# Gating values of a token mixer by seven block products instead of eight half products, with the spatial gate moved one stage later

## The chip, the cores and the metric

The kernel runs on one core of a Trainium2 chip. The metric is the device time of one execution in microseconds, the median of several runs. All matrix products work on 32-bit floats that are split into a high and a low part of the type fp32r ("hi" and "lo"), so that each product of two tiles is three matmuls: hi x hi, hi x lo and lo x hi.

## What is computed

The reference is one layer of a token mixer and a convolutional feed-forward part, for 512 tokens of width 1024 and 256 context tokens. What matters here is the token mixer, and in it u, vs and r:

```python
hx = _modulate(_rms_norm(x, norm1_g[l]), sh1x, sc1x)
z = h @ w_in
u, vs, q, r, ga, gb, k, v, lr = _split(z, IN_SPLITS)
a = _spatial_gating(gelu(u), gelu(vs), sgu_ln_g, sgu_ln_b, sgu_w, sgu_b)
...                                   # o: gated linear attention of q, k, v
ob = o.astype(h.dtype) * jax.nn.silu(r)
merged = sigmoid(ga) * (a @ w_br_a) + sigmoid(gb) * (ob @ w_br_b)

def _spatial_gating(u, vs, ln_g, ln_b, w_s, b_s):
    vn = _layer_norm(vs, ln_g, ln_b).reshape(bsz, n, SGU_CHUNK, SGU_GROUPS, SGU_GROUP_DIM)
    s = jnp.einsum('gpq,bnqgc->bnpgc', w_s, vn) + b_s.T[:, :, None]
    return u * s.reshape(bsz, length, SGU_WIDTH)
```

vs, r, ga and gb are each a product of the modulated x (512 x 1024) with 1024 columns of w_in (1024 x 1024). u is one too, but it is wanted with its channels on the partitions.

## The kernel before, in words

**Stages.** After the context's products and the products for q, k and v, the stages that matter here follow each other in this order: vs, u, the r gate, the ga gate, the gb gate, the product with w_br_a (also called a gate), the product with w_br_b, w_o, and the feed-forward part. The attention of four heads is cut into steps that run as hooks between the matmuls (`hook`, L1021); those of heads 2 and 3 run beside vs.

**Weights.** All weights come as a stream of units in the list `specs`: a unit is 512 KB, either all 1024 rows by 128 columns (u) or 256 rows by 512 columns (the others). `weights()` (L267) hands out the next unit. Its load on SP's queue goes to one of five raw buffers (RAW, L41); ACT casts it to its high part (L249) and DVE subtracts to get the low part (L250), into one of five pairs. So up to ten units can be ahead of the PE.

**vs** (`wide_tm`, L411, called at L1175): two halves of 512 columns, each with four token tiles of 128, eight blocks of the inner dimension and three matmuls of 128x512; 192 matmuls and eight units. `vs_done` (L1163) applies Gelu and collects the statistics of the layer norm. Behind it stand the mean, the variance and the normalisation (L1178 to L1190).

**u** (L1288): eight units, each with 24 matmuls (`prod_cm`, L392) and a Gelu. One step later `sgu_part` (L1249) does the spatial gate for this block of channels: four small matmuls with the turned spatial weights, an operation with bias on DVE (L1254), the product with u (L1256), and a spill to HBM on POOL's queue (L1246). `hx_sum` (L1261) runs in pieces in the same stage: it loads quarters of the modulated x back from HBM (L1265) and makes four sums of them for each of two blocks of the inner dimension, p1, s3, s2 and q4, each with a high and a low part (L1268 to L1273).

**A gate** (`gate`, L1365) is a product of 512 x 1024 with 1024 x 1024 by seven block products instead of eight, a scheme in the manner of Strassen and Winograd, applied to both halves of the inner dimension, which add up in PSUM. Each of the seven (`gate_product`, L1351) has two units and 24 matmuls. It needs sums of quarters of the activations (above) and sums of quarters of the weights. The order is a11, p1, s2, a21, s3, q4, a22; a11, a21 and a22 are read directly from hx, the quarter a12 is not read by itself. The seven results are combined by copies on ACT (L1343) and by DVE (L1348). Between the products `at` runs other work, and `ticks` (L1412) says how many steps of the background products with w_ada (`ada2`, L1196) run at each unit.

**Sums of the weights** (`sums_build`, L205) are made in HBM by DMAs on POOL's queue: for each weight and each of two blocks four copies (L214) and four accumulating DMAs (L216), 512 KB each. Each waits for the matmul that was last when it was traced. They are issued one at each unit (two at units 1 to 9, DENSE), at every second hook while the unit is below R_AT, and six beside the context's products (L1090). R_AT is the number of units before the first gate. Four weights have such sums: r, ga, gb and w_br_a, in this order; those of the feed-forward part's last product begin at unit SUMS0.

**Order and buffers.** Instructions are traced in program order; a scheduler of the framework places them by a cost model, subject to their data and to free buffers, except where `in_order` pins an order. The pools `heap` (43 buffers of 2 KB a partition) and `late` (26) hold nearly everything.

Of the kernel before, what the change touches and what calls it, by code (L numbers as in the profile page):

```python
# [16 lines left out]
P = 128  # L17
# [15 lines left out]
ENDS = 4  # L33
LEAD = 5
EARLY = 8
SUMS0 = 84
ADA2 = 7
DENSE = 10
SHSC = 6
# [5 lines left out]
def backbone_kernel(  # L45
# [39 lines left out]
    def const(shape, s, dt=F32):  # L85
        return cp.tile(shape, dt, tag=s, name=s)
# [57 lines left out]
    def w_cols(w, c0, n=P, k0=0, kn=KT):  # L144
        specs.append((w[k0 * P:(k0 + kn) * P, c0:c0 + n].rearrange("(k p) c -> p k c", p=P), kn, n))

    wi = w_in[0]
    for h in range(1, NH):
# [18 lines left out]
    def quarters(w, c0):  # L167
        return lambda b, row, col: w[(4 * b + 2 * row) * P:(4 * b + 2 * row + 2) * P,
                                     c0 + col * 512:c0 + (col + 1) * 512]
# [985 lines left out]

    vraw = [[None] * 4 for _ in range(2)]
    stats = const([P, 4, 2, 6], "stats")

    behind = []

    def vs_done(hf, t, ps):  # L1163
        vraw[hf][t] = (late if hf else heap)([P, 512], s="vr")
        A.activation(vraw[hf][t], ps, AF.Gelu)

        for h_, t_ in ((), ((), ((0, 0), (0, 1), (1, 0), (1, 1)), ((0, 2), (0, 3), (1, 2)), ((1, 3),))[t])[hf]:
            V.bn_stats(stats[:, t_, h_, :], vraw[h_][t_])
        if hf and t == 0:
            sgu_load()  # L1170
            behind.append(len(traced()))
        if hf and t == 1:
            in_order(behind.pop(), V.engine)

    wide_tm(hx, vs_done, hook)  # L1175
    while hooks:
        hook()
    mv = const([P, 4, 2], "mv")  # L1178
    for t in range(4):
        V.bn_aggr(mv[:, t, :], stats[:, t, :, :])  # L1180
    var = const([P, 5, 4], "var")
    V.tensor_scalar(var[:, 1:5, :], oss, 1.0 / 256, None, op0=ALU.mult)
    V.tensor_copy(var[:, 0, :], mv[:, :, 1])
    A.activation(var, var, AF.Sqrt, bias=eps_t, scale=1.0)
    V.reciprocal(var, var)
    vrs, ors = var[:, 0, :], var[:, 1:5, :]
    for hf in range(2):
        for t in range(4):
            z = vraw[hf][t]
            V.tensor_scalar(z, z, mv[:, t, 0:1], vrs[:, t:t + 1], op0=ALU.subtract, op1=ALU.mult)  # L1190


    bc_g = {}
    cols = {}

# [43 lines left out]
                V.reduce_sum(cols[kind][:, j * 4:j * 4 + 4], t_, axis=AX.X)  # L1239
            yield  # L1240

    a_kept, ob_kept = [], {}
# [6 lines left out]
    def sgu_part(j, ug):  # L1249
# [4 lines left out]
        V.scalar_tensor_tensor(s_, ps.rearrange("p (t r) -> p t r", t=4), lng[:, j:j + 1],  # L1254
                               sgb[j // 4][:, j % 4, :].unsqueeze(1).to_broadcast([P, 4, P]), op0=ALU.mult, op1=ALU.add)
        V.tensor_tensor(ug, s_.rearrange("p t r -> p (t r)"), ug, op=ALU.mult)  # L1256
        a_kept.append(spill(ug))

    hx_sums = {}

    def hx_sum(b):  # L1261
        def quad(i, hf):
            t_ = heap([P, 2, 256], s="fq")
            for kk in range(2):
                dma(t_[:, kk], fx_kept[4 * b + 2 * i + kk][:, hf * 256:(hf + 1) * 256])  # L1265
            return t_

        def kept(name, t_, p, q, op):  # L1268
            V.tensor_tensor(t_, p, q, op=op)
            pair = [pool([P, 2, 256], F32R, s="xs") for pool in (heap, late)]  # L1270
            A.copy(pair[0], t_)
            V.tensor_tensor(pair[1], t_, pair[0].bitcast(F32), op=ALU.subtract)
# [12 lines left out]
    pieces = [z for z in (hx_sum(0), hx_sum(1)) for _ in range(4)]  # L1285

    prev = None
    for j in range(KT):  # L1288
        if j:
            next(pieces[j - 1])  # L1290
        w = weights()
        ps = mm()
        prod_cm(ps, w, hx)
        ug = heap([P, S], s="ug")
        A.activation(ug, ps, AF.Gelu)
        if j < 2:
            for i in range(2):
                (sgu_turn, sgu_bias)[j](i)
        if prev is not None:
            sgu_part(*prev)  # L1300
        prev = (j, ug)
    next(pieces[-1])
    sgu_part(*prev)


    ob_t = {}
# [10 lines left out]
    r_sum = of_sums(lambda name, b: hx_sums[name, b])  # L1317

    def r_silu(src):
        z = late([P, 512], s="obt")  # L1320
# [41 lines left out]

    banks = []

    def gate(out, pool, at={}, mids=late, quad=r_quad, sum_=r_sum):  # L1365
# [24 lines left out]
        for t in range(2):  # L1390
            out(1, t + 2, combine(m5[t], X[t], ALU.subtract, pool))
        later(4)
        gate_product(Z, sum_("q4"))
        for t in range(2):
            out(1, t, combine(Z[t], u2[t], ALU.subtract, pool))
        later(5)
        gate_product(X, quad("a22"))
        later(6)
        for t in range(2):
            out(0, t + 2, X[t])  # L1400

    pending = []

# [494 lines left out]
```

## Time and profile before

| what | value |
|---|---|
| median of three runs | 907.68 us (907.58 to 908.59) |
| span of the profiled execution | 906.9 us |
| HBM read, written | 193.19 MB, 65.01 MB |
| DMA packets | 157291, 202.41 MB |
| DMA issues of sums, from w_in / from a sum | 36 / 26 of 512 KB, landing after 7.7 / 7.4 us in the median |
| ACT waiting for PE to free a split pair in the feed-forward part (wh L249) | 104.0 us |

PE is TensorE's matmuls and PEld its weight loads, DVE VectorE, ACT ScalarE, POOL GpSimd, SP SyncE, which issues most DMAs here. A row of the profile reads: engine, line, operation, output<-inputs, shapes, count, duration. A row of a stretch of time reads: start and end, length, busy time of each engine with its count of instructions, granted clock, DMA share (mean busy share of 16 DMA engines; it can exceed 1 where packets overlap) and GB/s.

### The profile page before, as it was taken

The numbers are of one execution on the slowest core, as the hardware profiler recorded it, in microseconds if no ns is written. First come the engines' busy times: TensorE is split into PE (matmuls) and PEld (weight loads), VectorE is DVE, ScalarE is ACT, GpSimd is POOL, SyncE is SP. The second block draws the span as 40 slices with busy tenths as digits, with TensorE's granted clock in tenths as the row PEclk, the third lists the DMA queues.
The fourth block names the chain that finished last, engine by engine and source line by source line (L and its number), as shares of the span: only waits on it lengthen the run. The fifth ranks groups of instructions, "written<-read, shape, count | busy, mean of one in ns | idle before, by whom it ended". The sixth has DMA issues, their size and how long they took to land.

```text
span 906.9 us, 12500 instructions
## 1 busy us (share of the span) xinstructions
PE 892.4 (98%) x4464; PEld 744.0 (82%) x4464; DVE 719.3 (79%) x1205; ACT 468.7 (52%) x778; POOL 98.6 (11%) x154
## 2 busy tenths in 40 slices
PE   7999999999999999999999999999999999999996
PEld 5778888888888888888888889888888888888885
DVE  6468687869786478688998868897899987896996
ACT  6256455747533557678531448433343434356763
POOL 1311231212112200000000010001111110000000
PEclk9999999999999999999999999999999999999998
DMA  9985996899979999886999651998998893256552
GB/s 278 346 275 158 265 272 120 170 315 156 241 254 245 245 294 330 262 282 190 361 367 350 202 169 38 287 299 180 191 218 179 175 196 96 89 167 207 174 183 96
DMA packets 157291, 202.41 MB, mean 223 GB/s; under 512 B 9465, under 2 KB 88645, under 8 KB 157229
## 3 DMA queue, kind: packets, MB, share of 16 engines
q1 hardware_dynamic: 131229, 137.39, 47.1%
q0 software_dynamic: 24160, 61.04, 30.4%
q10 hardware_dynamic: 1840, 3.18, 0.9%
q8 instruction: 35, 0.57, 0.3%
q14 instruction: 27, 0.22, 0.1%
HBM read 193.19 MB, written 65.01 MB: 285 GB/s over the span
## 4 chain that ended last, share of the span: by engine, by line
PE 95%; DVE 1%; ACT 1%; DMA 1%; SPq 0%; issue 0%; ACTq 0%
PE mm L390 33%; PE mm L408 15%; PE mm L1360 12%; PE gl L1795 10%; PE gl L1360 5%; PE gl L926 3%; PE mm L690 2%; PE gl L408 2%; PE mm L1795 2%; PE gl L690 1%; PE mm L1038 1%; PE mm L1088 1%; PE gl L599 1%; PE gl L961 1%; PE gl L1252 1%; DMA wa<-in_w_ada_dram 1%
## 5 line engine op out<-in xcount | busy, mean ns | idle before, releaser
L249 ACT CAST wh<-raw 128x1024 fp32r<-128x1024 f32 x183 | 189.0, 1036 | 201.3 <-PE mm L390 104.0
L250 DVE TENSOR_TENSOR wl<-raw,wh 128x1024 fp32r<-128x1024 f32 x183 | 218.3, 1199 | 71.6 <-ACT wh L249 63.0
L390 PE MATMUL mm<-h2h,wh 128*128 128x512 f32 (+1 forms) x344 | 133.0, 387 | 0.0
L390 PE MATMUL mm<-h2l,wh 128*128 128x512 f32 (+1 forms) x344 | 133.0, 387 | 0.0
L390 PE MATMUL mm<-h2h,wl 128*128 128x512 f32 (+1 forms) x344 | 133.0, 387 | 0.0
L1647 DVE SCALAR_TENSOR_TENSOR cacc<-ca,ccol,cacc 128x441 f32<-128x441 f32 (+2 forms) x176 | 121.8, 694 | 4.4
L390 PEld LDWEIGHTS mm<-h2h,wl 128*128 128x128 f32 x344 | 64.6, 188 | 13.2
L390 PEld LDWEIGHTS mm<-h2l,wh 128*128 128x128 f32 x344 | 64.6, 188 | 13.1
L390 PEld LDWEIGHTS mm<-h2h,wh 128*128 128x128 f32 x344 | 64.6, 188 | 13.0
L1795 PE MATMUL gl<-wh,dah 128*128 128x512 f32 x132 | 51.3, 389 | 0.0
L1795 PE MATMUL gl<-wl,dah 128*128 128x512 f32 x132 | 51.3, 389 | 0.0
L1795 PE MATMUL gl<-wh,dal 128*128 128x512 f32 x132 | 51.3, 389 | 0.0
L1216 DVE SCALAR_TENSOR_TENSOR acc<-wa,cs,acc 128x512 f32<-128x512 f32 x64 | 45.8, 744 | 0.0
L1648 ACT ACTIVATE cacc<-cacc 128x512 f32<-128x512 f32 x22 | 13.9, 633 | 59.2 <-DVE cacc L1647 59.1
L214 POOL DMA_DIRECT2D sum<-in_ffn_w_down_dram x24 | 13.2, 554 | 281.6 <-PE mm L408 184.5
L390 PE MATMUL mm<-hxh,wh 128*128 128x512 f32 x104 | 41.3, 397 | 0.0
L390 PE MATMUL mm<-hxl,wh 128*128 128x512 f32 x104 | 40.6, 390 | 0.0
L390 PE MATMUL mm<-hxh,wl 128*128 128x512 f32 x104 | 40.5, 390 | 0.0
L216 POOL DMA_DIRECT2D sum<-sum x28 | 25.2, 899 | 113.1 <-PE mm L390 49.6
L408 PE MATMUL mm<-wh,hxh 128*128 128x512 f32 x88 | 34.7, 395 | 0.0
L408 PE MATMUL mm<-wl,hxh 128*128 128x512 f32 x88 | 34.4, 391 | 0.0
L408 PE MATMUL mm<-wh,hxl 128*128 128x512 f32 x88 | 34.3, 390 | 0.0
(464 smaller groups left out, 2031.4 us busy)
## 6 DMA issues: line engine op xcount, KB each, us to landing
raw<-sum SPq DMA_DIRECT2D x52, 512.0 KB, 4.4
wa<-in_w_ada_dram SPq DMA_DIRECT2D x96, 256.0 KB, 6.2
raw<-in_w_in_dram SPq DMA_DIRECT2D x46, 512.0 KB, 5.8
raw<-in_ffn_w_up_dram SPq DMA_DIRECT2D x44, 512.0 KB, 5.5
sum<-in_w_in_dram POOLq DMA_DIRECT2D x36, 512.0 KB, 7.7
sum<-in_ffn_w_down_dram POOLq DMA_DIRECT2D x30, 512.0 KB, 6.5
sum<-sum POOLq DMA_DIRECT2D x26, 512.0 KB, 7.4
raw<-in_ffn_w_down_dram SPq DMA_DIRECT2D x15, 512.0 KB, 4.2
```

Of the source, the lines that this page charges most:

```text
L216: G.dma_start(sums[b][dst], ap, accum_op=ALU.add)
L249: A.copy(wh, raw)
L250: V.tensor_tensor(wl, raw, wh.bitcast(F32), op=ALU.subtract)
L390: T.matmul(ps, a[:, k, :], b[:, c0:c0 + n], start=(k == 0 and i == 0), stop=(k == KT - 1 and i == 2))
L408: T.matmul(ps, a[:, t * P:(t + 1) * P], b[:, k % 2, :], start=(k == 0 and i == 0), stop=(k == KT - 1 and i == 2))
L690: T.matmul(fps[i], a, b, start=(k == 0 and z == 0), stop=(k == KT - 1 and z == 2))
L926: T.matmul(ps, p_, q_, start=(start and z == 0), stop=(stop and z == 2))
L1216: behind_last(lambda: V.scalar_tensor_tensor(acc[i], coming.pop(0), cs[:, k, 0:1], acc[i], op0=ALU.mult, op1=ALU.add), V)
L1360: T.matmul(banks[t], a(kk, t), w[:, kk, :], start=(first and b == 0 and kk == 0 and i == 0), stop=(b == 1 and kk == 1 and i == 2), skip_gr ...
L1647: V.scalar_tensor_tensor(o, a_[:, r0 + dy:r1 + dy, c0 + dx:c1 + dx], wcol(tap), o, op0=ALU.mult, op1=ALU.add)
L1648: A.activation(acc, acc, AF.Gelu)
L1795: T.matmul(ps, a, w[:, kk, :], start=(first and kk == 0 and i == 0), stop=(last and kk == n_ - 1 and i == 2), skip_group_check=True)
```

## The change

vs becomes a gate and moves behind u. Its weights get sums of their own, the first that are built (80 sum DMAs for five weights, before 64 for four). u now runs where vs ran, with the attention's hooks beside it (one inside and one behind each of its eight products); Gelu(u) is spilled to HBM at once and loaded back later, three parts ahead. The spatial gate's eight parts run in the r gate, two each behind its second to fifth product, in the order 4 to 7 and 0 to 3. The sums of x are made at the end of u and beside the first three products of vs; q4 is no longer kept in buffers of its own but written over the quarter a12 of hx, which no gate reads. The first gate is now vs, so the copies that only the first gate makes move to it.

```diff
-SUMS0 = 84
+SUMS0 = 90
...
-    for hf in range(2):
-        for k in range(KT // 2):
-            w_cols(wi, O_VS + hf * 512, 512, 2 * k, 2)
     for j in range(KT):
         w_cols(wi, O_U + j * P)
     R_AT = len(specs)
...
-    gate_weights = [(quarters(wi, c0), sum_tiles(2)) for c0 in (O_R, O_GA, O_GB)]
+    gate_weights = [(quarters(wi, c0), sum_tiles(2)) for c0 in (O_VS, O_R, O_GA, O_GB)]
...
-    wide_tm(hx, vs_done, hook)
-    while hooks:
-        hook()
...
+    ug_kept, ug_back = [], {}
+
+    def ug_load(j):
+        ug_back[j] = heap([P, S], s="ug")
+        dma(ug_back[j], ug_kept[j])
+
+    def sgu_part(j):
+        ug = ug_back.pop(j)
         ps = gl()
...
-        a_kept.append(spill(ug))
+        a_kept[j] = spill(ug)
...
         kept("p1", a22, a21, a22, ALU.subtract)
         yield
+        kept("s2", a22, a22, a11, ALU.subtract)
+        yield
         kept("s3", a21, a11, a21, ALU.subtract)
         yield
-        kept("s2", a11, a22, a11, ALU.subtract)
+        V.tensor_tensor(a12, a12, a22, op=ALU.add)
+        for kk in range(2):
+            hi, lo = (z[:, 256:512] for z in hx[4 * b + kk])
+            A.copy(hi, a12[:, kk])
+            V.tensor_tensor(lo, a12[:, kk], hi.bitcast(F32), op=ALU.subtract)
         yield
-        kept("q4", a12, a12, a11, ALU.add)
-        yield
...
+    sums_of = [hx_sum(0), hx_sum(1)]
+
+    def piece():
+        for z in sums_of:
+            next(z)
+
     for j in range(KT):
-        if j:
-            next(pieces[j - 1])
         w = weights()
         ps = mm()
-        prod_cm(ps, w, hx)
+        for k in range(KT):
+            prod_k(ps, w, hx, k, 0, S)
+            if k == 3:
+                hook()
         ug = heap([P, S], s="ug")
         A.activation(ug, ps, AF.Gelu)
-        if j < 2:
-            for i in range(2):
-                (sgu_turn, sgu_bias)[j](i)
-        if prev is not None:
-            sgu_part(*prev)
-        prev = (j, ug)
-    next(pieces[-1])
-    sgu_part(*prev)
+        ug_kept.append(spill(ug))
+        hook()
+    while hooks:
+        hook()
+    sgu_load()
+    piece()
...
+    def vs_out(hf, t, src):
+        z = vraw[hf][t] = heap([P, 512], s="vr") if not hf and t > 1 else src
+        A.activation(z, src, AF.Gelu)
+        V.bn_stats(stats[:, t, hf, :], z)
+
+    def vs_step(i):
+        if i in (0, 1, 2):
+            piece()
+        if i in (0, 1):
+            sgu_turn(i)
+        if i in (3, 4):
+            sgu_bias(i - 3)
+        if i > 3:
+            ug_load(SGU_ORDER[i - 4])
+
+    SGU_ORDER = (4, 5, 6, 7, 0, 1, 2, 3)
+    ticks = [0] * 14
+    gate(vs_out, heap, {i: lambda i=i: vs_step(i) for i in range(7)}, late, pool1=late)
...
+    def sgu_step(i):
+        for n in ((), (0, 1), (2, 3), (4, 5), (6, 7), (), ())[i]:
+            sgu_part(SGU_ORDER[n])
+            if n + 3 < KT:
+                ug_load(SGU_ORDER[n + 3])
...
-    gate(r_out, heap, mids=heap)
+    gate(r_out, heap, {i: lambda i=i: sgu_step(i) for i in range(7)})
```

More of the change, by code (lines that the diff above doesn't have):

```diff
@@ L1154, in sgu_bias @@
                                    lnb[:, 4 * i + g:4 * i + g + 1], sgb[i][:, g, :], op0=ALU.mult, op1=ALU.add)
[L1158 to L1173, printed above, removed]
-    wide_tm(hx, vs_done, hook)
-    while hooks:
-        hook()
[L1178 to L1190, printed above, removed]
     bc_g = {}
@@ L1240, in ada2 @@
             yield
-    a_kept, ob_kept = [], {}
+    a_kept, ob_kept = {}, {}
     def spill(src, start=G.dma_start):
@@ L1315, in r_quad, with r_sum @@
                    for z in range(2)]
-    r_sum = of_sums(lambda name, b: hx_sums[name, b])
+    x_sum = of_sums(lambda name, b: hx_sums[name, b])
+    def r_sum(name):
+        return r_quad("a12") if name == "q4" else x_sum(name)
     def r_silu(src):
@@ L1363, in backbone_kernel, with gate @@
     banks = []
-    def gate(out, pool, at={}, mids=late, quad=r_quad, sum_=r_sum):
+    def gate(out, pool, at={}, mids=late, quad=r_quad, sum_=r_sum, pool1=None):
+        pool1 = pool1 or pool
         fresh = not banks
@@ L1390, in gate @@
         for t in range(2):
-            out(1, t + 2, combine(m5[t], X[t], ALU.subtract, pool))
+            out(1, t + 2, combine(m5[t], X[t], ALU.subtract, pool1))
         later(4)
@@ L1394, in gate @@
         for t in range(2):
-            out(1, t, combine(Z[t], u2[t], ALU.subtract, pool))
+            out(1, t, combine(Z[t], u2[t], ALU.subtract, pool1))
         later(5)
@@ L1400, in gate @@
             out(0, t + 2, X[t])
+    vraw = [[None] * 4 for _ in range(2)]
+    stats = const([P, 4, 2, 6], "stats")
+    def vs_out(hf, t, src):
[14 more added lines that the diff above has]
+    gate(vs_out, heap, {i: lambda i=i: vs_step(i) for i in range(7)}, late, pool1=late)
+    mv = const([P, 4, 2], "mv")
+    for t in range(4):
+        V.bn_aggr(mv[:, t, :], stats[:, t, :, :])
+    var = const([P, 5, 4], "var")
+    V.tensor_scalar(var[:, 1:5, :], oss, 1.0 / 256, None, op0=ALU.mult)
+    V.tensor_copy(var[:, 0, :], mv[:, :, 1])
+    A.activation(var, var, AF.Sqrt, bias=eps_t, scale=1.0)
+    V.reciprocal(var, var)
+    vrs, ors = var[:, 0, :], var[:, 1:5, :]
+    for hf in (1, 0):
+        for t in range(4):
+            z = vraw[hf][t]
+            V.tensor_scalar(z, z, mv[:, t, 0:1], vrs[:, t:t + 1], op0=ALU.subtract, op1=ALU.mult)
+    def sgu_step(i):
[3 more added lines that the diff above has]
+                ug_load(SGU_ORDER[n + 3])
     pending = []
```

3 lines of the change are left out of this document (removed).

## The prediction

> **What bounds the kernel now.** I read the head of the page and its chain first, then the busy time by stage, then the PE's timeline at a product's edge, then what the weights of the r gate waited for.
>
> ```profile
> span 906.9 us, 12500 instructions
> PE 892.4 (98%) x4464; PEld 744.0 (82%) x4464; DVE 719.3 (79%) x1205; ACT 468.7 (52%) x778; POOL 98.6 (11%) x154
> PE 95%; DVE 1%; ACT 1%; DMA 1%; SPq 0%; issue 0%; ACTq 0%
> ```
>
> The PE is busy for 98% of the span and 95% of the chain that ended last is PE. So a matmul taken away should shorten the kernel, as long as nothing else starts to hold the PE up. The profiled execution spans 906.9 us; the median of the runs is 907.68, so 0.8 us lie around the span.
>
> The stages that the change touches, in stretches of the trace (columns: stretch and length; busy us and instructions of PE, PEld, DVE, ACT, POOL; granted clock; DMA share; GB/s). They are vs, u, the r gate and the ga gate:
>
> ```profile
> 190.00:247.00 57.00, 57.00 (x328) 50.14 (x327) 47.46 (x110) 35.30 (x75) 10.00 (x14) 1.00 0.90 219
> 247.00:299.00 52.00, 52.00 (x265) 44.16 (x264) 36.12 (x61) 20.76 (x32) 8.93 (x14) 1.00 0.85 242
> 299.00:338.00 39.00, 39.00 (x177) 32.36 (x176) 24.41 (x32) 21.78 (x29) 5.68 (x7) 1.00 1.00 282
> 302.00:326.00 24.00, 24.00 (x108) 19.87 (x107) 11.51 (x13) 13.13 (x16) 3.86 (x5) 1.00 1.07 273
> 338.00:376.00 38.00, 38.00 (x177) 31.39 (x176) 30.95 (x39) 26.18 (x34) 0.00 (x0) 1.00 0.89 296
> ```
>
> The PE never waits, at full clock. But the 16 DMA engines are at 0.85 to 1.00 in these stages, and 1.07 for 24 us of the r gate. The second limit is close. How close, the last product of the r gate shows:
>
> ```profile
> 326.63 0.39 PE L1360 MATMUL gl<-wh,xs 128*128 128x512 f32 x1
> 332.07 0.39 PE L1360 MATMUL mm<-wh,hxh 128*128 128x512 f32 x1
> 328.62 1.05 ACT L249 CAST wh<-raw 128x1024 fp32r<-128x1024 f32 x1 [3.08 <-DMA raw<-sum]
> 329.70 2.51 DVE L250 TENSOR_TENSOR wl<-raw,wh 128x1024 fp32r<-128x1024 f32 x2 [2.04 <-ACT wh L249]
> DMA to landing us min/median/max: 7.5/9.9/14.1
> DMA to landing us min/median/max: 3.9/5.2/6.2
> ```
>
> The first two rows are the starts of the sixth and seventh product: 24 matmuls in 5.44 us, 227 ns each. (The mean of 0.39 us of one is its pipelined length, not its price.) ACT had waited 3.08 us for a weight load before it could split it, and the split of the seventh product's two weight units ended at 329.70 + 2.51 = 332.21, while that product began at 332.07 and needs its second unit six matmuls (1.36 us) later, at 333.43. A margin of 1.2 us is left. The buffers allow ten units in advance (RAW = 5 raw, and five split pairs of the pool wp), which is ten times 5.44 / 2 = 27 us; nearly all of it was eaten within one gate. The two landing rows are those of the weight loads, from 300 to 335 us, while sums are still being built on POOL's queue, and from 345 to 380 us, when none is: 9.9 against 5.2 us at the median.
>
> The Trainium skill, page "DMA: Bandwidth & Descriptors", section "Queues, rings and completion order", says that each DMA engine goes round the queues that have work for it, a packet at a time. The landings agree: the weights get no precedence over the sums. The chance of starvation below is set by the rows alone.
>
> **The change part by part.**
>
> *Matmuls.* vs goes from 2 halves x 4 token tiles x 8 x 3 = 192 matmuls of 128x512 to 7 products x 24 = 168. That removes 24 x 227 ns = 5.44 us from a PE that is full: **-5.4 us**. The 64 small matmuls of the spatial gate, 8 transposes and 4 bias matmuls move to vs and r and cost the PE what they did. The attention hooks that ran beside vs now run beside u, with the same 192 matmuls: nothing on PE.
>
> *DVE and ACT.* Rows for what is added or moved:
>
> ```profile
> L249 ACT CAST wh<-raw 128x1024 fp32r<-128x1024 f32 x183 | 189.0, 1036 | 201.3 <-PE mm L390 104.0
> L250 DVE TENSOR_TENSOR wl<-raw,wh 128x1024 fp32r<-128x1024 f32 x183 | 218.3, 1199 | 71.6 <-ACT wh L249 63.0
> L1168 DVE BATCH_NORM_STATS2 stats<-vr x8: 670/682/694, 218.8 to 244.1; 128x6 f32<-128x512 f32 x8
> L1190 DVE TENSOR_SCALAR vr<-vr,mv,var x8: 534/536/547, 249.9 to 253.1; 128x512 f32<-128x512 f32 x8
> L1254 DVE SCALAR_TENSOR_TENSOR sg<-gl,vec_b,sgb x8: 742/744/752, 262.1 to 301.7; 128x512 f32<-128x512 f32 x8
> L1256 DVE TENSOR_TENSOR ug<-sg,ug x8: 682/685/692, 263.4 to 302.5; 128x512 f32<-128x512 f32 x8
> L1265 SPq DMA_DIRECT2D fq<-fx x16: 319/451/1107, 249.1 to 280.6; - x16
> L1269 DVE TENSOR_TENSOR fq<-fq,fq x8: 678/682/693, 257.8 to 290.4; 128x512 f32<-128x512 f32 x8
> L1271 ACT CAST xs<-fq x8: 607/610/623, 259.5 to 299.0; 128x512 fp32r<-128x512 f32 x8
> L1272 DVE TENSOR_TENSOR xs<-fq,xs x8: 680/682/694, 260.2 to 300.5; 128x512 fp32r<-128x512 f32 x8
> DMA to landing us min/median/max: 5.6/6.1/6.7
> ```
>
> In the vs gate DVE has 14 unit splits (14 x 1.20 = 16.8 us), three sums of x for two blocks (6 x 1.36 = 8.2), q4 (about 3), eight statistics (5.4), six combines at the 0.68 of such a 128x512 operation (4.1) and the weights' turn and bias (about 5.5): 43 us beside some 40 us of PE. That is full, with up to 3 us late. In the r gate DVE had 24.4 us in 39 us; eight spatial parts add 8 x (0.744 + 0.685) = 11.4 and the normalisation 4.3, so 40 of 46 us: hidden. In u DVE loses the spatial parts and takes the attention's work, as vs did: hidden. The 3 us lie under the wait worked out next, which gives DVE time; alone they would cost 0 to 3 us. I add nothing.
>
> *Queues.* The ug spill on POOL now waits for the Gelu; behind it are sums that a later product releases anyway: nothing. The ug loads on SP wait for a heap slot, with weight loads behind them. The ten units in advance cover such a wait only if they are still there.
>
> *Transfers*, the term that decides. Prices, in us of all 16 engines:
>
> ```profile
> q0 software_dynamic: 24160, 61.04, 30.4%
> 690.00:745.00 55.00, 55.00 (x244) 45.57 (x243) 49.57 (x73) 21.50 (x29) 8.72 (x10) 1.00 0.94 190
> 755.00:800.00 45.00, 45.00 (x200) 37.24 (x200) 36.73 (x53) 17.26 (x24) 0.00 (x0) 1.00 0.30 94
> 820.00:880.00 60.00, 60.00 (x267) 49.67 (x266) 52.36 (x72) 40.32 (x61) 0.00 (x0) 1.00 0.55 176
> L216 POOL DMA_DIRECT2D sum<-sum x12: 812/878/881, 685.2 to 745.0; - x12
> L214 POOL DMA_DIRECT2D sum<-in_w_br_a_dram x5: 557/557/576, 247.2 to 273.6; - x5
> L216 POOL DMA_DIRECT2D sum<-in_w_br_a_dram x4: 910/914/939, 279.9 to 299.9; - x4
> L216 POOL DMA_DIRECT2D sum<-sum x4: 873/914/1224, 300.5 to 319.3; - x4
> ```
>
> A weight unit of 512 KB: 820 to 880 us has only those, one per 2.72 us, at share 0.55, so 0.55 x 2.72 = 1.5 us. An accumulating sum (line 216): 690 to 745 us has ten of them besides the loads that alone make 0.30, so (0.94 - 0.30) x 55 / 10 = 3.5 us. A copying sum (line 214): the software queue's 30.4% is 276 us, less 54 whole accumulates (190) and 16 spills (12), over 54 copies: 1.4 us. 256 KB: 0.75, half a unit. One of the 16 fq loads of 128 KB: 0.4.
>
> The sums are paced by the code: six in the context's products, one per weight unit, a second one in units 1 to 9, one per second hook while the unit is below R_AT. With 37 hook calls up to there, 19 of them odd, 6 + 18 + 8 + 19 = 51 of now 80 are issued when the vs gate begins (unit 18, the new R_AT). So 28 fall into vs and r: by the order of each weight's 8 copies and 8 accumulates, 13 copies and 15 accumulates. In the kernel before, u and r had five and eight (last three rows).
>
> After, vs and r: 28 units 42, 15 accumulates 52.5, 13 copies 18.2, 16 fq 6.4, and 28 pieces of 256 KB (8 ug loads, 8 a spills, 4 spatial weights, some 8 w_ada) 21: 140 us. The same count for u and r before gives 22 x 1.5 + 28 + 7 + 6.4 + 12 = 86, where the trace shows 0.85 x 52 + 1.00 x 39 = 83; by that ratio 140 becomes 135. The PE's time for vs and r is 52 + 39 - 5.4 = 86 us, and at the highest share held for long (1.07) the engines do 92 us of work in it. 43 are too many. The ten units in advance may be used up: 15 us. That leaves 28 us of work, 26 us of time, if the sums keep pace; if three accumulates (10.5 us) trail into the ga gate, 16 us. Ga itself has (1.07 - 0.89) x 38 = 7 us to spare, and without units in advance some bursts there will show too: 0 to 5. Between 16 and 31 I take 22, nearer the low end since the last sums are not read until w_br_a's gate. **PE wait +22 us.**
>
> Sum: -5.4 + 22 = +16.6, so span 923.5 and **924.3 us** for the median. Its own range: share 1.11 and trailing sums give about 13 us of wait (915), share 1.0 and the bursts 36 to 40 (942).
>
> **The rivals.**
>
> *It all fits* (faster). If bytes rather than accumulates priced the engines, the 28 + 28 half-megabytes, fq 2.1 MB and 7.3 MB of pieces are 38.8 MB; at the best rate of the trace,
>
> ```profile
> 440.00:470.00 30.00, 30.00 (x134) 24.86 (x133) 30.00 (x42) 13.79 (x18) 0.59 (x1) 1.00 1.05 404
> ```
>
> that is 96 us, less 13 for the units in advance: 83, under the PE's 86. Then only the matmuls count: 902.3 us. For it: the PE never waited so far. Against it: the stretch at 190 GB/s that already fills 0.94. The Trainium skill's page named above, section "Anatomy of one DMA", prices the moving part at bytes over 436 GB/s; by that estimate 38.8 MB take 89 us and this case would hold; the 3.5 us of an accumulate speak against it, as here 512 KB come to 150 GB/s. Chance 0.24.
>
> *Only the first sum is late.*
>
> ```profile
> 246.66 0.28 PE L926 MATMUL gl<-vh,ptl 128*128 128x256 f32 x1
> 249.10 7.64 SPq L1265 DMA_DIRECT2D fq<-fx  x8
> ```
>
> p1 of both blocks must be ready when the first vs product ends, 5.44 us after u. Before, the first eight fq loads left from 249.10 us, 2.2 us after the attention's last product (246.66 + 0.28), whose end frees buffers; they cost SP 0.45 us each, landed 6.1 us later, and 1.97 us of sub, cast and sub follow. For the second block, whose needed quarters are the ninth to twelfth loads, that is 2.2 + 12 x 0.45 + 6.1 + 2.0 = 15.7 us, 10 us too late; less if buffers free earlier. With the rest fitting: 905 to 912. In the forecast this wait is not added, since the engines work on through it. Chance 0.16.
>
> *The sums starve the weights*, the forecast: 0.60.
>
> **How the numbers follow.** A change of 0.2% (1.8 us) is about what a measurement of this kernel can tell. Fits is all faster: 0.24. The late first sum straddles the bound: 0.06 same, 0.10 slower. The forecast is slower. Faster 0.24, same 0.06, slower 0.70. The range must leave out at most 2 in 10: from 902 (most of the fitting case) to 944; the likeliest case alone has 915 to 942.
>
> **What would show it.** 24 fewer matmuls; between 247 us and the end of r, 15 to 30 us of PE idle, put down to splits (wl, wh) that waited for raw; weight loads landing after 10 us or more there; a DMA share of 1.0 or more through both gates; sums of w_br_a landing into ga. If PE idles under 3 us there and raw lands in 5 to 8 us, the ledger of the engines is wrong. If the idle stands in one piece before the second vs product, the first sum is the cause.

## The result and the profile after

| | before | after |
|---|---|---|
| median | 907.78 us (907.58 to 908.59, four runs) | 938.96 us (936.26 to 939.68, four runs) |
| span of the profiled execution | 906.9 us | 938.0 us |
| matmuls | 4464 | 4440 |
| mean granted clock | 0.997 | 0.982 |

The ratio is 1.0333, with a 95% interval of 1.0317 to 1.035. All of it arises between 180 us and the second product of the ga gate, which starts at 342.95 us before and at 373.91 after (30.96 us later); the offset hardly changes from there to the end.

The head of the page after, its clock row (PEclk: the granted clock in tenths, in 40 equal slices of the span) and its chain by engine:

```profile
span 938.0 us, 12560 instructions
PE 898.9 (96%) x4440; PEld 744.6 (79%) x4440; DVE 728.9 (78%) x1217; ACT 487.7 (52%) x800; POOL 115.1 (12%) x178
PEclk9999999999989797999999999999999999999999
PE 81%; DMA 10%; ACT 3%; DVE 3%; SPq 2%; issue 1%; DVEq 0%; ACTq 0%
```

The PE's share of the chain fell from 95% to 81%, and DMA, 1% before, has 10%. Two slices of the clock row have 7 and one has 8: here the PE was not only late but slow.

The same by stage, with the columns of the prediction's stretches: the u products, the vs gate, the r gate, and the ga gate as far as it was disturbed:

```profile
195.50:252.50 57.00, 53.28 (x298) 46.47 (x297) 38.99 (x89) 42.43 (x75) 13.34 (x19) 0.97 0.84 215
252.50:301.60 49.10, 44.48 (x183) 34.19 (x181) 31.80 (x52) 21.74 (x36) 8.93 (x13) 0.93 0.91 266
301.60:358.50 56.90, 49.20 (x234) 40.63 (x232) 37.92 (x58) 26.42 (x34) 13.96 (x21) 0.91 1.07 347
358.50:408.70 50.20, 42.34 (x186) 34.71 (x186) 33.83 (x43) 27.08 (x36) 4.17 (x5) 0.90 1.01 312
```

Before, the second column was equal to the length in every stage and the clock was 1.00. Now each stage loses some us of PE, and each a tenth or less of its clock. Who the PE waited for stands in the waits from 180 to 470 us (engine, tile and line that waited, releaser: us in total, times, the longest):

```profile
PE mm L1338 <- DVE wl L247: 15.6, 3, 7.9
PE gl L1338 <- ACT xs L1240: 3.8, 2, 3.4
PE gl L941 <- ACT junk L1010: 3.7, 1, 3.7
PE mm L1338 <- ACT wh L246: 0.7, 1, 0.7
ACT wh L246 <- DMA raw<-in_w_in_dram: 26.2, 9, 9.6
ACT wh L246 <- DMA raw<-sum: 14.9, 7, 4.2
DVE stats L1387 <- ACT dc L1386: 11.2, 4, 7.3
DVE ug L1225 <- DMA ug<-kept: 11.6, 3, 8.6
```

The first four rows are the PE's own: 15.6 us for the low parts of weights, 3.8 for the first sum of x, 3.7 for a step of the attention in u, 0.7 for a high part: 23.8 us. The other rows show what ACT and DVE were waiting for meanwhile.

**What adds up.** The matmuls give -5.4 us and the stops +23.8. The clock: (1 - 0.982) x 938.0 = 16.9 us of full-speed time was not granted, against (1 - 0.997) x 906.9 = 2.7 before, so 14.2 more; what fell on a standing PE cost nothing. Together 32.6 us, or less by what of the slow clock fell on a standing PE, against 31.1 measured.

**How one late load becomes a stop.** In the timelines ACT and DVE take their instructions in a fixed order, also when one that stands further back could run. The timeline of ACT ahead of the largest stop of the r gate:

```profile
292.09 1.05 ACT L246 CAST wh<-raw 128x1024 fp32r<-128x1024 f32 x1 [1.56 <-DMA raw<-in_w_in_dram]
293.05 0.63 ACT L1386 ACTIVATE dc<-dc 128x512 f32<-128x512 f32 x1
303.25 1.04 ACT L246 CAST wh<-raw 128x1024 fp32r<-128x1024 f32 x1 [9.58 <-DMA raw<-in_w_in_dram]
304.20 0.62 ACT L1386 ACTIVATE dc<-dc 128x512 f32<-128x512 f32 x1
```

and of DVE in the same time:

```profile
296.30 1.22 DVE L247 TENSOR_TENSOR wl<-raw,wh 128x1024 fp32r<-128x1024 f32 x1
304.86 0.69 DVE L1387 BATCH_NORM_STATS2 stats<-dc 128x6 f32<-128x512 f32 x1 [7.34 <-ACT dc L1386]
305.47 0.67 DVE L1326 TENSOR_TENSOR dc<-gl,dt 128x512 f32<-128x512 f32 x1
306.06 1.22 DVE L247 TENSOR_TENSOR wl<-raw,wh 128x1024 fp32r<-128x1024 f32 x1
```

The cast at 303.25 waited 9.58 us for its load. Behind it on ACT stood a Gelu of vs (L1386), behind that Gelu on DVE its statistics (L1387), and behind these, at 306.06, the low part of the unit *before* the late one, whose high part had been ready since 293.14 (292.09 + 1.05). The PE needed that one first. So the late load held up its predecessor, and the unit that had landed gave no reserve.

The stop in the ga gate has the same shape with another load at its head, that of u (L1215, issued at 344.2 us; DVE's wait for it ended at 363.9). Two units that ACT had already cast, at 352.22 and 357.94 us, stood behind it on DVE:

```profile
354.63 0.69 DVE L1225 TENSOR_TENSOR ug<-sg,ug 128x512 f32<-128x512 f32 x1
363.93 0.69 DVE L1225 TENSOR_TENSOR ug<-sg,ug 128x512 f32<-128x512 f32 x1 [8.61 <-DMA ug<-kept]
364.54 0.69 DVE L1326 TENSOR_TENSOR dc<-gl,dt 128x512 f32<-128x512 f32 x1
365.14 1.22 DVE L247 TENSOR_TENSOR wl<-raw,wh 128x1024 fp32r<-128x1024 f32 x1
```

**And what follows a stop.** The PE at the end of the r gate's stop (start, length, and in brackets the idle time before):

```profile
307.33 0.80 PE L1338 MATMUL mm<-wl,hxh 128*128 128x512 f32 x1 [5.39 <-DVE wl L247]
307.93 0.63 PE L1338 MATMUL mm<-wh,hxl 128*128 128x512 f32 x1
308.35 0.63 PE L1338 MATMUL mm<-wh,hxh 128*128 128x512 f32 x1
```

From 307.93 on the matmuls start 0.42 us apart instead of 0.227. The stretches of the trace in which the granted clock was half:

```profile
220.84:224.25 3.41, 3.41 (x11) 2.97 (x12) 0.88 (x2) 3.36 (x5) 0.59 (x1) 0.50 0.82 150
268.62:275.45 6.83, 5.65 (x13) 4.03 (x14) 5.69 (x9) 2.11 (x4) 0.00 (x0) 0.50 0.80 283
306.17:316.41 10.24, 6.76 (x15) 4.88 (x16) 7.62 (x12) 6.15 (x9) 2.03 (x3) 0.50 1.09 298
360.79:371.03 10.24, 4.62 (x11) 3.65 (x12) 7.10 (x11) 5.05 (x7) 2.44 (x3) 0.50 0.88 229
```

In them the PE was busy for 3.41 + 5.65 + 6.76 + 4.62 = 20.4 us at half speed, which is 10.2 us lost (with these in place of the 14.2, the sum above is 28.6). The Trainium skill, page "TensorE: Matmul & The Clock Gate", Part 1, says that the clock falls to half after an idle window of about 3.4 us and that the windows run on by themselves. The trace agrees on the windows: the stretches are one, two and three times 3.41 us, and their starts lie 47.78, 37.55 and 54.62 us apart, which is 14, 11 and 16 times 3.413. It does not agree that a window must be idle as a whole; the last section has the numbers.

### The profile page after: what moved, and what is told of

Read it like the earlier page. It is cut to its first block, busy times and chain, and to the rows that moved or that the text cites. A ratio compares the mean times of both kernels' runs of the same rounds, so it can differ in the third digit from the quotient of the medians.

```text
span 938.0 us, 12560 instructions
## 1 busy us (share of the span) xinstructions
PE 898.9 (96%) x4440; PEld 744.6 (79%) x4440; DVE 728.9 (78%) x1217; ACT 487.7 (52%) x800; POOL 115.1 (12%) x178
## 2 busy tenths in 40 slices
DMA packets 164044, 218.15 MB, mean 233 GB/s; under 512 B 10073, under 2 KB 89253, under 8 KB 163981
## 3 DMA queue, kind: packets, MB, share of 16 engines
q0 software_dynamic: 28128, 71.53, 33.1%
## 4 chain that ended last, share of the span: by engine, by line
PE 81%; DMA 10%; ACT 3%; DVE 3%; SPq 2%; issue 1%; DVEq 0%; ACTq 0%
PE mm L387 31%; PE mm L405 11%; PE mm L1338 10%; PE gl L1815 10%; DMA raw<-sum 5%; PE gl L1338 4%; DMA ug<-kept 2%; PE gl L923 2%; PE mm L687 2%; PE mm L1815 2%; DMA fq<-fx 2%; PE mm L1035 1%; PE mm L1085 1%; PE gl L405 1%; DMA sgb<-in_sgu_b_dram 1%; SPq L297 1%
## 5 line engine op out<-in xcount | busy, mean ns | idle before, releaser
L246 ACT CAST wh<-raw 128x1024 fp32r<-128x1024 f32 x189 | 194.8, 1037 | 212.8 <-PE mm L387 89.2
L247 DVE TENSOR_TENSOR wl<-raw,wh 128x1024 fp32r<-128x1024 f32 x189 | 225.6, 1202 | 59.0 <-ACT wh L246 58.6
L1338 PE MATMUL mm<-wl,hxh 128*128 128x512 f32 x96 | 40.2, 419 | 15.6 <-DVE wl L247 15.6
L213 POOL DMA_DIRECT2D sum<-sum x32 | 28.1, 889 | 124.7 <-PE mm L387 60.8
L1338 PE MATMUL mm<-wh,xs 128*128 128x512 f32 x128 | 41.5, 395 | 0.0
L1338 PE MATMUL mm<-wh,hxh 128*128 128x512 f32 x96 | 39.6, 416 | 0.8 <-ACT wh L246 0.7
```

The source lines that it names most:

```text
L213: G.dma_start(sums[b][dst], ap, accum_op=ALU.add)
L246: A.copy(wh, raw)
L247: V.tensor_tensor(wl, raw, wh.bitcast(F32), op=ALU.subtract)
L1338: T.matmul(banks[t], a(kk, t), w[:, kk, :], start=(first and b == 0 and kk == 0 and i == 0), stop=(b == 1 and kk == 1 and i == 2), skip_gr ...
```

## The experiments

Times of one run each stand without an interval; the kernel before had medians of 907.8 to 908.5 us beside them. Where a kernel with stops was run more than once, its runs lay 0.9 to 8.0 us apart, so a few us between single runs decide nothing. All edits are to the kernel after, unless another is named.

**Do the sums starve the weights?** Two kernels make the sums cheaper, or fewer at that time. The first issues the accumulating DMAs as copies:

```diff
-                    if len(step) == 4:
+                    if plain or len(step) == 4:
...
-            yield from sums_build(*z)
+            yield from sums_build(*z, plain=True)
```

> The changed kernel, but the accumulating DMAs of the gate weights' sums are issued as plain copies of the same rows, in the same order and number (the additions of the 40 accumulates are left out, so the gates multiply by other weights). Theory (the accumulating sums fill the DMA engines and starve the weight loads): each accumulate falls from 3.5 to about 1.4 us of all 16 engines, 15 of them in the vs and r gates, so 31 us less engine work there; the three waits for raw in r and ga shrink from 15.6 us to under 4, the half clock behind them goes, about 910 to 922 us; the first sum's 4.5 us and the attention's 3.7 us in u stay. Rival (the engines are priced by bytes, the waits come from the order of the queues): 939 us, the same waits.

The second spreads them:

```diff
-            for _ in range((i >= at) + (at <= i < DENSE)):
+            for _ in range((i >= at) + (at <= i < DENSE) if at > 1 or i < R_AT or i % 2 else 0):
```

> The changed kernel, but from the first vs unit on only every second weight unit issues a step of the gate weights' sums; it computes the whole reference. 14 steps move out of the vs and r gates into those behind. Theory (sums starve the weights): 14 steps of 1.4 to 3.5 us are 35 us less engine work in vs and r, so the waits for raw there and their half clock go: 908 to 920 us, with some of it given back if ga and gb, at shares of 0.9 before, have no room. Rival (the waits come from the reload of u, the spatial parts and the first sum, whatever the sums do): 930 us or more.

Measured: 920.58 and 920.22 us, one run each. By two different ways 18 of the 31 us go. The landing times of the weight loads issued from 285 to 345 us, first of the kernel after, then of the plain copies, then of half pace:

```profile
DMA to landing us min/median/max: 11.7/15.2/20.0
```

```profile
DMA to landing us min/median/max: 6.5/7.0/13.9
```

```profile
DMA to landing us min/median/max: 7.4/10.3/14.3
```

With plain copies, the PE's wait for low parts and the stretch of r are

```profile
PE mm L1338 <- DVE wl L247: 2.8, 2, 2.4
```

```profile
301.60:358.50 56.90, 54.55 (x267) 46.12 (x267) 47.25 (x73) 29.64 (x39) 12.29 (x22) 0.97 1.02 387
```

The wait for weights fell from 15.6 to 2.8 us (2.8 at half pace too). With plain copies the whole kernel has as many DMAs and moves the same 218.15 MB; over this stretch it moves 387 GB/s where the kernel after moved 347, and loads land in half the time. So the price lies in accumulating, not in the bytes that the profile counts. The bytes rival falls. The results stand near the upper ends of what the theory gave, 920.58 inside 910 to 922 and 920.22 just above 908 to 920; the first sum and the stop in u were left in both.

The pages of the profile also give the price itself. The packets of the software queue, which carries the sums, took 33.1% of the span of 938.0 us in the kernel after and 27.4% of 918.9 with plain copies: 58.7 us for 40 accumulates, so an accumulate costs 1.5 us more than a copy, where the prediction's rows had 2.1 us between them (3.5 and 1.4).

A third kernel leaves the 16 sum steps of the vs weights out:

```diff
-    gate_weights = [(quarters(wi, c0), sum_tiles(2)) for c0 in (O_VS, O_R, O_GA, O_GB)]
+    gate_weights = [(quarters(wi, O_VS), [[quarters(wi, O_VS)(b, 0, 1)] * 4 for b in range(2)])]
+    gate_weights += [(quarters(wi, c0), sum_tiles(2)) for c0 in (O_R, O_GA, O_GB)]
...
-        for z in gate_weights:
+        for z in gate_weights[1:]:
```

> The changed kernel without the 16 sum steps of the vs weights: the vs gate reads raw quarters of the same size in their place (the sums of those weights are left out), everything else as changed. Theory (the vs block sums are what overfills the engines): 8 copies and 8 accumulates are 39 us of engine work less; with 51 steps done when vs begins 13 are left for vs and r instead of 29, so it comes out near the half-pace kernel: 914 to 920 us. Rival (the moved work, the spill and reload of u and the sums of x in the gate, is what overfills them): 930 us or more.

Measured: 931.17 us, a miss. The accumulates on POOL's queue from 280 to 312 us (count, durations, first and last start):

```profile
L214 POOL DMA_DIRECT2D sum<-in_w_br_a_dram x4: 872/1073/1258, 283.6 to 287.6; - x4
L214 POOL DMA_DIRECT2D sum<-sum x4: 878/878/878, 293.1 to 310.9; - x4
```

and the PE's wait for low parts:

```profile
PE mm L1339 <- DVE wl L248: 7.3, 2, 4.2
```

With 16 steps fewer, the accumulates that remain moved forward: eight of them, those of w_br_a, now lie between 283.6 and 310.9 us, in the place where the kernel after has eight of gb's (281.5 to 308.4). The two stops there come to as much, 7.3 us against 5.39 + 2.32 = 7.7; the one in the ga gate is gone. This speaks for the pace of accumulates over some 25 us as what decides, not their sum over two stages: the stages as a whole stood at shares of only 0.87 and 0.93. That the moved work alone would fill the engines, as the rival had it, isn't shown by its number coming out.

**The reload of u.** It is left out, and the result multiplied by itself:

```diff
-        dma(ug_back[j], ug_kept[j])
...
-        V.tensor_tensor(ug, s_.rearrange("p t r -> p (t r)"), ug, op=ALU.mult)
+        V.tensor_tensor(ug, s_.rearrange("p t r -> p (t r)"), s_.rearrange("p t r -> p (t r)"), op=ALU.mult)
```

> The changed kernel without the eight loads of u back from HBM: the spatial part multiplies its own result by itself (the product with u is left out). The DVE can no longer stand before that multiply. Theory A (the 7.9 us stop in the ga gate is the DVE blocked by one late load of u, with weight splits queued behind it): that stop and the 10 us of half clock behind it (5 us of time) go, the stops of 5.4 and 2.3 us in r stay or shrink a little: 923 to 931 us. Theory B (the load was late only as everything was, the engines' work decides): 8 loads of 256 KB are 6 us of engine work, 932 to 937 us, with the weights' wait in ga in another place.

Measured: 930.95 us, the upper end of theory A. One run, 1 us from what theory B gave, but the waits speak for A: the stop of 7.9 us in ga is gone (stops of at most 0.8 us are left there), DVE waits for no load of u, and in r one stop of 3.6 us for weights is left of the 5.4 and 2.3, beside a new one of 1.9 us for a spatial part on DVE.

**The stop in u.** u is copied, without its Gelu:

```diff
-        A.activation(ug, ps, AF.Gelu)
+        A.copy(ug, ps)
```

> The changed kernel with u taken out of PSUM by a plain copy on ACT (the Gelu of u is left out). Theory (ACT, which now alternates between the Exp of the attention and the Gelu of u, loads a function table at each turn and holds the attention's products up): the 3.7 us stop in u and the 3.4 us of half clock behind it (1.7 us) go, ACT's table loads in u with them: 932 to 936 us. Rival 1 (the transfers behind u decide the end of vs and r, and the time won in u is lost in a longer wait there): 937 to 940 us, with the stops in vs and r longer by as much. Rival 2 (the stop is the turn of work on the DVE or the PE's order, not the tables): 939 us, the stop in u still there.

Measured: 931.45 us (930.5 to 932.63), ratio to before 1.0258 (1.0241 to 1.0275): 7.5 us less, slightly more than forecast. The stage of u, which had 53.28 us of PE at a clock of 0.97, is whole:

```profile
195.50:252.50 57.00, 57.00 (x323) 49.90 (x322) 40.41 (x93) 32.19 (x71) 14.69 (x21) 1.00 0.95 249
```

ACT's ten table loads there are gone too. What they were shows the timeline of ACT in the kernel after:

```profile
205.74 1.28 ACT L880 ACT_TABLE_LOAD   x1
207.03 1.15 ACT L880 ACTIVATE lx<-lx 128x512 f32<-128x512 f32 x2
208.20 1.28 ACT L882 ACT_TABLE_LOAD   x1
```

L880 is Exp, L882 is Ln: six of the ten loads stand at Exp and Ln, four at the Gelu. In the kernel before, the first Gelu of vs came behind them (one table load, at 214.65 us), and the table that the kernel loads at 0.80 us lasted until then, for Exp and for Ln. The first Gelu of u, at 188.37 us, replaces it, and after that Exp and Ln each fetch a table. The Trainium skill, page "ScalarE: Activation LUTs", section "Table sets: the hidden batching unit", says that one set holds both functions; the trace of the kernel before agrees, in that Exp and Ln alternate there without a load. The page gives about 2.7 us for a load; here a load took 1.28 us, and the functions on both sides stand within 0.02 us of it.

Two attempts to have this gain in a kernel that computes everything failed, and say why. First the Gelu on the way back, with half pace:

```diff
-        A.activation(ug, ps, AF.Gelu)
+        A.copy(ug, ps)
...
+        A.activation(ug, ug, AF.Gelu)
         V.tensor_tensor(ug, s_.rearrange("p t r -> p (t r)"), ug, op=ALU.mult)
```

> The half-pace kernel, and u leaves PSUM by a plain copy and is put to HBM so; its Gelu is taken when it comes back, just ahead of the multiply. It computes the whole reference. Theory (ACT's ten table loads of 1.28 us in the u products, one for each turn between the attention's functions and the Gelu, made the 3.7 us stop and its 3.4 us of half clock): both go, 918.5 - 5.4 = 913 us of span, 912 to 915, if the gates behind have room. Rival (the transfers decide where vs and r end): the time comes back there as waits for raw, 917 to 920 us.

Measured: 928.56 us (928.02 to 928.92), worse than half pace alone (920.22, one run) and above what both sides had given. The stop in u is gone, but ACT now stands before the loads of u, with the casts behind it:

```profile
ACT ug L1225 <- DMA ug<-kept: 12.8, 3, 7.6
```

The rival had the time coming back in the gates, which it did, but its reason (waits for raw) was not it: ACT waited 16.7 us for raw, less than the 38.7 at half pace. On this kernel two more were built. One issues the loads of x ahead of those of the spatial weights:

```diff
-    sgu_load()
-    piece()
+    piece()
+    sgu_load()
```

> The kernel with half pace and the Gelu of u on the way back, and besides the first pieces of the sums of x (their loads from HBM) are issued ahead of the four loads of the spatial weights and bias on SP's queue. Theory (the first sum waits for its loads behind the bias load of 9 us): the stops of 0.4 to 3.4 us before the second vs product shrink to under 0.5, 1 to 2 us less than the kernel beside it, since at half pace only 0.5 to 1 us of them is left. Rival (the loads wait for buffers that the attention frees late, or for their share of the engines): no change within 0.5 us.

Measured: 924.28 us, one run. The stops around the first vs products were 1.14, 0.92 and 1.19 us, all for weights, where the kernel beside it had 0.70 for a weight and 1.67 for the sum: the sum came in time, and the weights behind its loads came later. The 4 us less come from the stops further on and are not explained. The other has this edit too and spreads the sums more:

```diff
-DENSE = 10
+DENSE = 14
...
-            for _ in range((i >= at) + (at <= i < DENSE) if at > 1 or i < R_AT or i % 2 else 0):
+            for _ in range((i >= at) + (at <= i < DENSE) if at > 1 or i < R_AT or (i % 2 if i > 45 else i % 3 == 0) else 0):
```

> As the kernel with the sums of x first, and the gate weights' sums spread further: a second step in units 1 to 13 instead of 1 to 9, one step every third unit in the vs and r gates, every second one behind. It computes the whole reference. Theory (the 2.4 us stop in r with its 3.4 us of half clock that half pace left is still the sums): it goes, another 3 to 4 us, 906 to 910 us, and the floor of 902 (the matmuls alone) is missed by what the later gates give back. Rival (ga and gb, at 1.05 of the engines already, starve instead, or the sums of w_br_a come too late for their gate): 912 to 920 us, with waits for raw from 370 us on.

Measured: 922.92 us (919.80 to 923.79), above both ends; ACT stood 17.5 us before loads of u, so the question of the third pace was not answered.

Second, the Gelu of four units put off to the fifth, before the spill, with half pace:

```diff
+    LATER, waiting = 4, []
...
-        A.activation(ug, ps, AF.Gelu)
-        ug_kept.append(spill(ug))
+        (A.copy(ug, ps) if j < LATER else A.activation(ug, ps, AF.Gelu))
+        waiting.append(ug)
+        if j >= LATER:
+            for z in waiting[:-1]:
+                A.activation(z, z, AF.Gelu)
+            ug_kept.extend(spill(z) for z in waiting)
+            waiting.clear()
```

> The half-pace kernel, and the Gelu of the first four units of u is put off: they leave PSUM by a copy, and their Gelu is taken in SBUF together with the fifth unit's, before the spill. It computes the whole reference; nothing is left to do when u comes back. Theory (table turns of ACT made the stop in u; the kernel with the Gelu on the way back lost the gain only because ACT then stood before loads of u): two or three table loads instead of ten, no stop in u, 5 us less than 918.5: 912 to 915 us of span. Rival (whatever is won in u is lost in the gates behind): 917 to 922 us.

Measured: 925.19 us (922.78 to 926.78), a miss: nine table loads, and a stop of 5.6 us in u. The framework's scheduler had placed the Gelus as soon as their data were there, among the Exp and Ln. The last kernel holds them back (below).

**More raw buffers.**

```diff
-LATE = 26
+LATE = 25
-AHEAD = 4
+AHEAD = 5
...
-RAW = 5
+RAW = 6
```

> The changed kernel with six buffers for raw weights instead of five and loads issued one unit further ahead (one buffer fewer in the late pool), nothing else. Theory A (a load lands late, 14 us, and with five under way that is 2.8 us a unit, just over the PE's 2.72; the queues of ACT and DVE hand one late load on to the split before it): six under way are 2.3 us a unit, the stops of 5.4 and 2.3 us in r and the 10 us of half clock there go, 926 to 932 us. Theory B (the engines are full, more loads under way only land later): loads land after 16 us or more, the same stops within 1 us, 937 to 940 us.

Measured: 935.17 us, one run, between the two. Its loads from 285 to 345 us and waits:

```profile
DMA to landing us min/median/max: 14.8/16.3/17.0
PE mm L1338 <- DVE wl L247: 7.4, 2, 5.5
```

The loads landed later (16.3 us at the median after 15.2), as theory B had it, and the 5.4 us stop stayed; those behind it shrank, and new ones of 1 to 2 us, for spatial parts on DVE, came up in r. A deeper buffer alone bought little here: 3.8 us between a single run and a median whose own runs lay 3.4 us apart.

**All together**, first with the Gelus where the scheduler put them, then held back:

> Half pace, the Gelu of the first four units of u put off, and six buffers for raw weights; it computes the whole reference. If each holds by itself, 5.4 us of u's stop and clock and some 4 of the stop of 2.4 us in r with its clock go from 918.5: 907 to 911 us, level with the kernel before. If the gates are held by the loads of u (on which DVE waits with the splits behind it) and not by raw, the last 4 us stay: 911 to 915 us.

Measured: 926.43 us (921.30 to 929.29), a miss, and no better than without the sixth buffer. In its profile the gates hardly wait for weights (0.6 us for low parts), but u still has its stop of 5.6 us. The last kernel differs from it in one thing:

```diff
+            after = next(z for z in reversed(traced()) if z.engine == T.engine)
+            start = len(traced())
             for z in waiting[:-1]:
                 A.activation(z, z, AF.Gelu)
+            for i in traced()[start:]:
+                if i.engine == A.engine:
+                    tc.add_manual_dep(i, after.name, ...)
```

> The kernel with half pace, six raw buffers and the Gelu of u put off, but the Gelus of the first four units are now held until the fifth unit's last product, so that they stand behind the last Exp and Ln of the attention on ACT (without that they stood among them, and nine table loads were left). It computes the whole reference. Theory (one Gelu ahead of the attention costs it the table that holds Exp and Ln together, and each turn between those two is then a load of 1.28 us): one table load between 180 and 255 us, no stop in u, and 5.6 us with 6.8 us of half clock (3.4) less than the 922.9 us span of the kernel that differs in nothing else: 914 us, 911 to 917. Rival (the gates behind take back what u wins): the stop in u gone and 919 us or more.

Measured: 919.92 us (914.17 to 921.21), span of the profiled execution 916.2, ratio to before 1.0119 (1.0097 to 1.0142). There is one table load between 180 and 253 us,

```profile
L1274 ACT ACT_TABLE_LOAD x1 | 1.3, 1283 | 0.0
```

no stop in u, and the median is 6.5 us lower than with the Gelus among the Exp and Ln. So the table is the cause of that stop: when the Gelu is taken is the only difference. The theory gave a span of 911 to 917 us: the profiled one lies in it, the median of the six spans, 918.2, 1.2 us above it, near the rival's 919. So part of the gain is given back. What is left is mainly this:

```profile
DVE ug L1225 <- DMA ug<-kept: 11.3, 3, 4.8
PE mm L1351 <- DVE wl L247: 3.4, 1, 3.4
PE mm L405 <- DVE sga L1534: 2.0, 1, 2.0
```

DVE standing before the loads of u with the splits behind it, a stop in the product with w_br_b, and 1.6 us for the first sum. No kernel with vs as block products came under the 907.8 us of the kernel before. Some 3 us of the last one's 9.3 us over it (916.2 less 906.9), beyond these stops, their clock and the 5.4 us gained, are not placed.

The gains of the single edits, 18 us for the sums, 8.0 for the reload and 7.5 for the table, come to more than the 31 us that were lost. They overlap: the stop in ga goes with plain copies as it goes without the reload.

## Why the prediction was right, and where it was not

The direction, the reason and the range held: 938.96 us in 902 to 944, and in the likeliest case's own 915 to 942. The point, 924.3, was 14.7 us too low, and that the range held without a term for the clock or the tables was in part luck.

- **Matmuls, -5.4 us.** 24 fewer, as said; PE x4440.
- **The ledger of the engines.** That an accumulate costs more than a copy is borne out by the plain copies, which gave back 18 us at equal bytes; the price was high, with 2.1 us above a copy for the 1.5 that the packet time shows. 14 copies and 12 accumulates were issued in vs and r, and four accumulates in ga (13 and 15 forecast, three of them to trail). The share in r was the forecast 1.07, but in vs it was 0.91: there the engines weren't full, since sums wait for products and a standing PE holds them back too (one accumulate waited 16.2 us for the PE). The ledger says whether two stages fit; it does not say where a stop falls, as the kernel without the vs sums showed.
- **PE wait, +22 us.** The stops came to 23.8, but not as forecast: 15.6 us for weights, just under the lower end of 16; 3.8 for the first sum, which was left out because the engines would work on through it (the rival had up to 10); 3.7 in u, which no step had; 0.7 for a high part. So 8.2 of the 23.8 came from places that the sum put at nothing, and that the total came so near was luck. Between 247 us and the end of r there were 12 us of stops, less than the 15 that the text set as its lower mark; the largest lay in ga.
- **Queues: nothing added for the loads of u, since ten units in advance would cover a wait on SP if they were still there.** This step failed. The load of u was the head of the largest stop, by way of DVE's order and not of SP's; leaving it out was worth 8 us. The reserve did not help: one late instruction on ACT or DVE held the split of units that had landed, one in r and two in ga.
- **DVE and ACT, "I add nothing".** In u the Gelu and the attention's functions met on ACT. The prediction weighed DVE's work there and had no term for ACT's tables: ten loads of 1.28 us where these functions had needed one; 7.5 us in all.
- **What was missing: the clock.** Every stop was priced at its length. After each of the larger ones the PE ran at half clock for 3.4 to 10.2 us: 10 to 14 us in all, which is most of the 14.7 by which the point was low.

Of the rivals, "it all fits" is out: 512 KB accumulated don't cost what 512 KB copied cost. "Only the first sum is late" was there, as a part of 3.8 us, on top and not instead.

## What to carry to other kernels

When transfers are moved into a stage, count for each in-order engine what stands behind an instruction that waits for a load: a reserve of landed units is worth nothing if their last step is queued behind someone else's load. Price a stop of the PE with the slow clock behind it, here 10 to 14 us on top of 24; a stop that took less than some half of a 3.41 us window cost no slow clock here. Moving an activation function past others can cost more in table loads than the functions themselves; look at which one comes first.

## What the runs showed of the hardware

The clock fell to half after stops shorter than the 3.4 us of one window. In the kernel with plain copies the PE stood for 1.94 us,

```profile
268.82 0.50 PE L1338 MATMUL gl<-wh,xs 128*128 128x512 f32 x1 [1.94 <-ACT xs L1240]
```

and 1.3 us after that stop's end, with the PE at work, the half clock began:

```profile
270.08:273.49 3.41, 3.41 (x9) 2.65 (x8) 3.17 (x5) 0.35 (x2) 0.00 (x0) 0.50 1.02 394
```

In the kernel with u copied, a stop of 2.60 us at the same place left the clock at 1.00. So the length of a stop alone does not say whether the slow clock follows. The Trainium skill's page "TensorE: Matmul & The Clock Gate", Part 1, has the windows run on without regard to the kernel. The traces show that the stop's place among them decides. The starts of a trace's half-clock stretches tell where its windows begin. In the kernel with u copied the end of a window cut the stop in two: of the two windows around that end, 1.14 and 1.69 us were without a matmul, and neither was followed by half clock:

```profile
258.75:262.17 3.42, 2.27 (x9) 1.23 (x7) 0.45 (x2) 1.66 (x3) 1.11 (x2) 1.00 1.05 386
262.17:265.58 3.41, 1.73 (x8) 1.43 (x9) 3.17 (x5) 2.11 (x4) 0.00 (x0) 1.00 1.04 406
```

With plain copies the shorter stop lay in a single window, the last one before the half clock:

```profile
266.67:270.08 3.41, 1.47 (x6) 1.05 (x6) 2.70 (x5) 1.93 (x4) 0.00 (x0) 1.00 1.05 401
```

The traces of the kernel after and of all twelve experiments agree, from 180 to 500 us: each of the 38 full-clock windows with 1.8 us or more without a matmul was followed by half clock, none with 1.54 us or less was, and of the six between one was. So about half of a window without matmuls was enough. This is read from the traces; no run moved a stop to try it.

The kernels with stops also repeat less well: the six runs of the last one spread over 7.0 us, those of the kernel before over 1 to 3. Where a stop falls among the windows may be part of that; it was not tried.
